# Half of two projections moved from plain tiles into a Strassen group of a decoder layer

## The chip, the cores and the metric

One core of a Trainium2 chip. The time is the device time of one execution in microseconds; before's is the median of three runs. The kernel works in fp32, and every product is made of three matmuls on operands split into a high and a low part.

## The reference

A hybrid decoder layer on 512 tokens of width 2048:

```
z = rms_norm(x) @ w_in                 # q k v g_attn c_b c_c c_h g_conv
y_attn = window_attention(q, k, v, sinks) * silu(g_attn)
y_conv = c_b * conv3(c_c * c_h) * silu(g_conv)
x = x + concat(y_attn, y_conv) @ w_out
x = x + sigmoid(rms_norm(x) @ w_ple_gate + b) * rms_norm(p @ w_ple_proj)
```

q has 16 heads and k and v have 4, of width 64; a query sees 128 keys. g_attn, c_b, c_c, c_h and g_conv are 1024 wide each. conv3 is a causal convolution over three tokens with weights of its own for each channel.

## The kernel before, in words

**Plain tiles.** k and v come first (L276). Then 8 tiles of q and 16 tiles of c_c and c_h are made by gemm_tile: one tile is 128 output columns by 512 tokens, 16 steps over the width with three matmuls each (mm3, L155 to L157), so 48 matmuls into a PSUM bank psg. Channels lie on the partitions and tokens along the free side. The weights of four steps are one split: ACT casts them to wh (L117), DVE takes the residue wl (L118); splits are prepared three ahead.

**The clock of that stage.** gemm_tile calls tick() after every second step, so a tile is 8 ticks of six matmuls. at(when, fn) hangs work on a tick; TensorE runs exactly in the order in which the program issues it, while a scheduler sets the order of the other engines here. The work hung on ticks: the turning of k and v, the sums of squares of q's heads (half_sums, L205) and the scale from them (head_scale, with a power step on POOL, L229), and attention.

**Attention** is 16 units (4 key heads by 4 blocks of 128 queries; the first block of a head has half the keys). scores (at `when`): 8 matmuls into pss, four passes on DVE that scale, mask and take the minimum (L457), four exponentials on ACT (L462), the sums, and the scaling of the rows, two on ACT (L472) and two on DVE (L474). turn (6 ticks later): transposes into pst, a cast on ACT (L487) and a residue on DVE (L488). values (9 ticks later): matmuls into pso, a copy to `up` and two stores by POOL's queue. pss and pso have one buffer, pst two. In before q ends at tick 64, and the units start 4 ticks later, 7 ticks apart, beside the c tiles.

**q tiles** cost DVE a shuffle, two rotary products, an add, a residue of the squares and two residues of q (L340 to L343, L131, L436). e_block (a small projection) sits in the middle of four of them, E_AT. h_forms prepares, for one eighth of the width, the sums of blocks of x that the next stage needs, and stores them by POOL's queue (8 sets, one behind each of eight tiles).

**c tiles.** For a pair of tiles, DVE makes zc = c_c times the squared inverse norm (L664), u = zc * c_h (L670), ACT the first tap (L672) and DVE two more (L674); the result goes to conv_dram. The last pair is finished behind the stage.

**Strassen groups.** The rest is 7 groups: three over w_mid (c_b with g_conv twice, then g_attn), two over w_out, two over w_ple_gate. A group makes 1024 columns for 512 tokens by the seven products of Strassen's scheme on 2 x 2 blocks: 28 steps (PER) of 12 matmuls (run_step, L846). Here tokens lie on the partitions. Each step needs a split of 128x1024 (L812 on ACT, L813 on DVE, two steps ahead) and some of them a sum of weight blocks (L794 to L800, or an adding DMA by POOL's queue, add_block). From here on every engine runs in the order of the program; soon(before or after, step) hangs work on a step. `quarters` joins the products into the four quarters of a group; conv_group and attn_group then turn them back to channels on partitions (turn, L912, 16 transposes in two calls).

Of the kernel before, what the change touches and what calls it, by code (L numbers as in the profile page):

```python
# [35 lines left out]
def hymba_layer(ctx: ExitStack, tc: tile.TileContext, io):  # L36
# [268 lines left out]
    with ExitStack() as att:  # L305
# [107 lines left out]
        def q_tile(t):  # L413
            ps = product()
            sq = split_tile(squares(ps))

            def sum_q():
                if t % 4 == 0:
                    tok["q"] = ps_o.tile([P, T], F32, name="pso")
                half_sums(tok["q"], sq, t % 4, t % 4 == 0, t % 4 == 3)  # L420
                if t % 4 == 3:
                    tok["q"] = take_rows(tok["q"], 8)

            def scale_q():
                sl = nscale[:, :, 2 * t - 6 : 2 * t + 2]
                head_scale(tok["q"], sl, tok["x", -1], nc.gpsimd)()

            at(clock[0] + 6, sum_q)
            if t % 4 == 3:
                at(clock[0] + (9 if t == 3 else 17), scale_q)  # L430
            qr = rotate(ps, qg)
            for hf in range(2):
                own, oth = slice(hf * HD, hf * HD + HD), slice((1 - hf) * HD, (1 - hf) * HD + HD)
                st = big.tile([P, T], F32R, tag="big", name="qst")
                nc.scalar.copy(st[own], qr[own])
                nc.vector.tensor_tensor(st[oth], qr[own], f32(st[own]), op=ALU.subtract)  # L436
                qst[2 * t + hf] = st
# [223 lines left out]
        for i in range(8):  # L661
            ps = product()
            zc = cw.tile([P, T], F32, tag="cw", name="zc", bufs=4) if i < 7 else rowp.tile([P, T], F32, tag="rows", name="zc")
            tt(zc, ps, rx2, op=ALU.mult)  # L664
            if i == 7:
                break
# [39 lines left out]

    groups = [(io["w_mid"], n) for n in range(3)] + [(io["w_out"], n) for n in range(2)] + [(io["w_ple_gate"], n) for n in range(2)]
    NG = len(groups)
    chunks = [(0, 1, 2, 3)] * 3 + [(0, 1, 3, 2), (0, 1, 2, 3), (0, 1, 3, 2), (0, 1, 3, 2)]
    LATE = (3, 5)  # L710
    T1_BY_DMA, T3_BY_DMA = range(1, NG - 1), (2, 3, 4)
    steps = []
# [13 lines left out]
    PER = len(steps) // NG  # L726
    HS, MIX, GATE = 0, 3 * PER, 5 * PER

# [90 lines left out]
    def run_step(s, forms):  # L819
# [10 lines left out]
        if start and first:  # L830
            if (g, acc) == (NG - 1, "a"):
                ps = [ps_t.tile([P, T], F32, name="pst") for _ in range(2)]
            else:
                ps = ps_abc[("abc".index(acc) + g) % 3].tile([P, 2, T], F32, name="psp")
                if g >= 5:
                    ps = [ps[:, b] for b in range(2)]
            psum[g, acc] = ps
        ps = psum[g, acc] if g >= 5 else [psum[g, acc][:, b] for b in range(2)]
        wh, wl = weights[s]
# [20 lines left out]
        else:  # L860
            for t in range(2):
                products(t)
        if g in (2, 4, 6):
            for i in range(2):
# [64 lines left out]
    def quarters(g, qs, s0):  # L929
# [12 lines left out]
        soon(after, s0 + 26, lambda: join(qs[0, 0], g, "c", ALU.add))  # L942

    def conv_group(g):
        s0, q, yc = g * PER, {}, []
# [12 lines left out]
        def load_y(i):  # L958
            yc.append(itile("yc"))
            nc.sync.dma_start(yc[i], conv_dram[4 * g + i])  # L960

        def evict(j, i, pt):
            y = yc[2 * j + i]
            tt(y, pt, y, op=ALU.mult)
            nc.gpsimd.dma_start(mix_dram[4 * g + 2 * j + i], y)

# [63 lines left out]
    def out_group(g):  # L1030
        s0, first = g * PER, 2 * (g - 3)

# [54 lines left out]

    s1, s2 = 4 * PER, 5 * PER
    for j, when, plan in (
# [27 lines left out]
    def gate_group(g):  # L1117
# [3 lines left out]
        def load_b():  # L1121
            ext["b"] = itile("gb")
            nc.sync.dma_start(ext["b"], io["b_ple_gate"][2 * (g - 5)][:, 0])

# [6 lines left out]
        def add_b(t, n):  # L1131
            nc.gpsimd.dma_start(q[t, n], io["b_ple_gate"][2 * (g - 5) + n], accum_op=ALU.add)

# [11 lines left out]
        def load_e(t, n, tile=itile):  # L1145
            ext[t, n] = [tile("e") for _ in range(2)]
            for b in range(2):
                nc.sync.dma_start(ext[t, n][b], e_dram[t][2 * (g - 5) + n][:, b])

# [7 lines left out]
        def add_x2(t, n):  # L1157
            nc.gpsimd.dma_start(q[t, n], x2_dram[t][2 * (g - 5) + n], accum_op=ALU.add)

        def store(t, n):  # L1160
            nc.gpsimd.dma_start(part(out, t, 2 * (g - 5) + n), q[t, n])

# [20 lines left out]
        soon(after, s0 + 22, load_b)  # L1183
        soon(after, s0 + 22, load_e, 0, 0, itile if g == 5 else spare)

        def new_z():
            q[1, 0] = qtile("z")

        if g == 5:
            soon(after, s0 + 26, join, 0, 0, "c", r_2)  # L1190
# [47 lines left out]
    attn_group(2)  # L1238
    out_group(3)
    out_group(4)  # L1240
    gate_group(5)
    gate_group(6)


# [6 lines left out]
    def last_conv():  # L1251
        tt(u, ps, zc, op=ALU.mult)
        nc.vector.tensor_scalar(y, u, convw[:, 2, 7:], None, op0=ALU.mult)
        for s in (1, 0):
            n = 2 - s
            stt(y[:, n:], u[:, : T - n], convw[:, s, 7:], y[:, n:], op0=ALU.mult, op1=ALU.add)
        nc.gpsimd.dma_start(conv_dram[7], y)

# [45 lines left out]
def _layout(inputs):  # L1304
# [15 lines left out]
    def cols(v):  # L1320
# [60 lines left out]
```

## Time and profile before

| | us |
|---|---|
| runs | 939.81, 940.88 (median), 943.29 |
| profiled execution, time | 940.36 |
| its span on the core | 938.6 |

The profile is of one execution. Busy time of a group is what its instructions cover together; a mean is the duration of one, and neighbours on an engine overlap a little. "Idle before" is what the engine waited in front of them, with what ended the wait. The chain that ended last is followed back from the last instruction.

### The profile page before, as it was taken

What the parts mean: (1) busy time and instruction counts of PE and PEld (TensorE: products, weight loads), DVE (VectorE), ACT (ScalarE), POOL (GpSimd) and SP (SyncE); (2) the same over time, 40 slices, a digit from 0 to 9 for tenths busy, and PEclk for the clock granted to TensorE, in tenths of its full rate; (3) what the DMA queues carried; (4) which work ended last, traced back from release to release, by engine and by line L of the source; (5) the groups of instructions that cost most, each with busy time, mean ns of one, the idle gap of its engine ahead of it and who ended that gap; (6) DMA issues with size and microseconds to landing.
All of it is one profiled execution on the core that took longest, in us unless ns stands there. A gap on an engine that the chain in (4) does not pass through costs nothing.

```text
span 938.6 us, 12350 instructions
## 1 busy us (share of the span) xinstructions
PE 929.7 (99%) x4292; PEld 773.0 (82%) x4292; DVE 714.9 (76%) x1108; ACT 525.2 (56%) x891; POOL 147.3 (16%) x196
## 2 busy tenths in 40 slices
PE   9999999999999999999999999999999999999997
PEld 7888888888888888888888888888888888888885
DVE  6778868875766676668667768989768696999777
ACT  7646555665656665245444446655556576665442
POOL 2002142051212221000100120011120112001101
PEclk9999999999999999999999999999999999999999
DMA  8434456454554667865924887785996995578757
GB/s 313 154 104 157 146 185 228 160 164 128 131 167 145 181 179 238 306 202 178 248 90 142 255 222 239 239 234 159 292 331 182 227 293 146 135 236 268 180 135 212
DMA packets 67502, 186.12 MB, mean 198 GB/s; under 512 B 8080, under 2 KB 14528, under 8 KB 67440
## 3 DMA queue, kind: packets, MB, share of 16 engines
q1 hardware_dynamic: 46192, 128.47, 40.2%
q0 software_dynamic: 21104, 56.86, 26.0%
q8 instruction: 33, 0.54, 0.2%
q14 instruction: 29, 0.24, 0.1%
q10 hardware_dynamic: 144, 0.01, 0.0%
HBM read 155.95 MB, written 29.36 MB: 197 GB/s over the span
## 4 chain that ended last, share of the span: by engine, by line
PE 96%; DVE 2%; issue 1%; DMA 0%; ACT 0%; SPq 0%; DVEq 0%; ACTq 0%
PE psp L846 51%; PE psg L155 9%; PE psg L157 9%; PE psg L156 9%; PE pst L846 3%; PE pss L276 2%; PE pst L276 2%; PE pst L912 1%; PE pst L482 1%; PE pss L556 1%; PE pst L556 1%; PE pss L450 1%; PE pss L449 1%; PE pso L497 1%; PE pso L496 1%
## 5 line engine op out<-in xcount | busy, mean ns | idle before, releaser
L846 PE MATMUL psp<-wh,form 128*128 128x512 f32 x1056 | 326.5, 390 | 0.3 <-DVE form L578 0.3
L846 PEld LDWEIGHTS psp<-wh,form 128*128 128x128 f32 x1056 | 197.4, 188 | 41.0 <-DVE form L578 0.7
L846 PE MATMUL psp<-wl,form 128*128 128x512 f32 x528 | 205.5, 389 | 0.0
L155 PE MATMUL psg<-hsh,wh 128*128 128x512 f32 x384 | 152.2, 396 | 0.0
L157 PE MATMUL psg<-hsh,wl 128*128 128x512 f32 x384 | 149.8, 390 | 0.0
L156 PE MATMUL psg<-hsl,wh 128*128 128x512 f32 x384 | 149.8, 390 | 0.0
L813 DVE TENSOR_TENSOR wl<-wy,wh 128x1024 fp32r<-128x1024 f32 x84 | 102.6, 1222 | 45.5 <-ACT wh L812 44.9
L812 ACT CAST wh<-wy 128x1024 fp32r<-128x1024 f32 x84 | 88.3, 1051 | 79.6 <-PE psp L846 61.4
L118 DVE TENSOR_TENSOR wl<-raw,wh 128x512 fp32r<-128x512 f32 x120 | 82.3, 688 | 46.3 <-ACT wh L117 28.4
L846 PEld LDWEIGHTS psp<-wl,form 128*128 128x128 f32 x528 | 99.1, 188 | 20.6
L117 ACT CAST wh<-raw 128x512 fp32r<-128x512 f32 x120 | 73.6, 616 | 65.0 <-PE psg L156 51.4
L813 DVE TENSOR_TENSOR wl<-wx,wh 128x1024 fp32r<-128x1024 f32 x56 | 68.4, 1223 | 31.9 <-ACT wh L812 31.7
L812 ACT CAST wh<-ws 128x1024 fp32r<-128x1024 f32 x56 | 59.1, 1055 | 59.1 <-PE psp L846 34.6
L812 ACT CAST wh<-wx 128x1024 fp32r<-128x1024 f32 x56 | 58.8, 1052 | 57.9 <-PE psp L846 49.4
L813 DVE TENSOR_TENSOR wl<-ws,wh 128x1024 fp32r<-128x1024 f32 x56 | 68.5, 1222 | 23.7 <-ACT wh L812 23.6
L157 PEld LDWEIGHTS psg<-hsh,wl 128*128 128x128 f32 x384 | 72.1, 188 | 15.5
L155 PEld LDWEIGHTS psg<-hsh,wh 128*128 128x128 f32 x384 | 72.2, 188 | 14.0
L156 PEld LDWEIGHTS psg<-hsl,wh 128*128 128x128 f32 x384 | 72.2, 188 | 13.8
L846 PE MATMUL psp<-wh,hsh 128*128 128x512 f32 x192 | 75.0, 391 | 0.0
L846 PE MATMUL psp<-wl,hsh 128*128 128x512 f32 x192 | 74.7, 389 | 0.0
L846 PE MATMUL psp<-wh,hsl 128*128 128x512 f32 x192 | 74.7, 389 | 0.0
L798 DVE TENSOR_TENSOR wy<-wy,ws 128x1024 f32<-128x1024 f32 x56 | 68.2, 1218 | 0.0
(223 smaller groups left out, 1351.3 us busy)
## 6 DMA issues: line engine op xcount, KB each, us to landing
raw<-in_w_in SPq DMA_DIRECT2D x48, 512.0 KB, 3.6
ws<-in_w_mid SPq DMA_DIRECT2D x24, 512.0 KB, 4.3
h<-hf POOLq DMA_DIRECT2D x32, 256.0 KB, 4.3
wx<-in_w_mid SPq DMA_DIRECT2D x16, 512.0 KB, 4.5
wx<-in_w_out SPq DMA_DIRECT2D x16, 512.0 KB, 6.4
ws<-in_w_out SPq DMA_DIRECT2D x16, 512.0 KB, 5.4
ws<-in_w_ple_gate SPq DMA_DIRECT2D x16, 512.0 KB, 5.0
wy<-in_w_mid SPq DMA_DIRECT2D x12, 512.0 KB, 6.2
```

Source lines behind the costliest of these rows:

```text
L117: nc.scalar.copy(wh, raw)
L118: nc.vector.tensor_tensor(wl, raw, f32(wh), op=ALU.subtract)
L155: nc.tensor.matmul(ps, wh, ah, start=first, stop=False)
L156: nc.tensor.matmul(ps, wh, al, start=False, stop=False)
L157: nc.tensor.matmul(ps, wl, ah, start=False, stop=last)
L276: nc.tensor.matmul(kv_ps[t], w[:, t, :], a, start=k == 0 and i == 0, stop=k == KT - 1 and i == 2)
L449: nc.tensor.matmul(sc[:, r, lo:], q, khh[j][:, ks], start=True, stop=False)
L556: nc.tensor.matmul(banks[t], a, w, start=k == 0 and i == 0, stop=k == 1 and i == 2)
L798: tt(y, y, got[g, "s1" if f == 6 else "s0", c], op=ALU.add)
L812: nc.scalar.copy(wh, src)
L813: tt(wl, src, f32(wh), op=ALU.subtract)
L846: nc.tensor.matmul(ps[t], a, w[:, i], start=start and first and i == 0 and n == 0, stop=last and i == 1 and n == 2, skip_group_check=not s ...
```

## The change

The second halves of c_c and c_h (4 tiles each) leave the plain tiles and become a Strassen group of their own, the first of now eight: its left 512 columns are c_c, its right 512 are c_h. square_group joins the quarters, multiplies c_c by c_h and the squared inverse norm token by token on DVE (L952 in the changed kernel), turns the product to channels (turn at steps 30 and 32, that is in the next group's third and fifth step), and takes the convolution straight from PSUM: ACT the last tap, DVE the two others in place (L960, L963), then a store to conv_dram by POOL's queue.

With 8 c tiles less there are 56 ticks fewer for attention. Its units now start at tick 46, inside q's tiles, 6 ticks apart up to the fourth, then from tick 67 on 42/11 ticks apart. The forms (h_forms) come behind tiles 0 to 5, 9 and 12, and e_block one tile earlier. Indices of groups move up by one.

```
-    E_AT = (2, 3, 4, 5)
+    E_AT = (1, 2, 3, 4)
...
-            at(c0 + 36 + 16 * t, finish_v)
+            at(c0 + 36 + 8 * t, finish_v)
...
-        busy[0] = [load_p]
-        for j, i in enumerate((4, 6, 7, 11, 14, 16, 18, 20)):
+        load_p()
+        for j, i in enumerate((0, 1, 2, 3, 4, 5, 9, 12)):
             busy.setdefault(i, []).append(lambda j=j: h_forms(j))
+        for u in range(NKV * NB):
+            attention(u // NB, u % NB, c0 + (46 + 6 * u if u < 4 else 67 + 42 * (u - 4) // 11))
         for t in range(8):
             q_tile(t)
-        t0 = clock[0] + 4
-        for u in range(NKV * NB):
-            attention(u // NB, u % NB, t0 + 7 * u)
-        for i in range(8):
+        for i in range(4):
             ps = product()
...
-    groups = [(io["w_mid"], n) for n in range(3)] + ...
+    groups = [(io["w_mid"], n) for n in range(4)] + ...
...
+    def square_group(g):
+        s0, q = g * PER, {}
+        quarters(g, q, s0)
+        def times(t, src):
+            for b in range(2):
+                stt(q[t, 0][:, b], src()[:, b], column(rx2_tok, t, b), q[t, 1][:, b], op0=ALU.mult, op1=ALU.mult)
+        def last():
+            q[1, 0] = qtile("z")
+            times(1, lambda: psum[g, "a"])
+        def evict(f, pt):
+            y = itile("yconv")
+            nc.scalar.activation(y, pt, AF.Copy, scale=convw[:, 2, f : f + 1])
+            for s in (1, 0):
+                n = 2 - s
+                stt(y[:, n:], pt[:, : T - n], convw[:, s, f : f + 1], y[:, n:], op0=ALU.mult, op1=ALU.add)
+            nc.gpsimd.dma_start(conv_dram[f], y)
+        soon(after, s0 + 27, times, 0, lambda: q[0, 0])
+        soon(after, s0 + 28, last)
+        for j in range(2):
+            soon(after, s0 + 30 + 2 * j, lambda j=j: turn(
+                j, (q[0, 0], q[1, 0]), lambda i, pt: evict(4 + 2 * j + i, pt)))
...
-    conv_group(0)
+    square_group(0)
     conv_group(1)
...
-        "w_mid": blocks(columns(TCB, TGC, TCB + 4, TGC + 4, TGA, TGA + 4)),
+        "w_mid": blocks(columns(TCC + 4, TCH + 4, TCB, TGC, TCB + 4, TGC + 4, TGA, TGA + 4)),
```

How the order of instructions moves is shown at three places. The first is DVE's queue ahead of the second attention unit's scores (ptl_a is the residue of unit 0's turned block, prob the scores); before:

```order
L118 TENSOR_TENSOR wl<-raw,wh 128x512
L664 TENSOR_TENSOR zc<-psg,rows_xx 128x512
L118 TENSOR_TENSOR wl<-raw,wh 128x512 x2
L488 TENSOR_TENSOR ptl_a<-pst,pth_a 128x512
L457 ISA prob,negm<-pss,mask,nsink,nscale 128x256
```

And now:

```order
L490 TENSOR_TENSOR ptl_a<-pst,pth_a 128x512
L580 TENSOR_TENSOR hf<-g,hf 128x512
L580 TENSOR_TENSOR hf<-g,hf 128x256
L340 STREAM_SHUFFLE shf<-psg 128x512
L131 TENSOR_TENSOR sl<-sqh,sh 128x512
L341 SCALAR_TENSOR_TENSOR rot<-psg,q_norm_gain,cos 128x512
L342 SCALAR_TENSOR_TENSOR shf<-shf,q_norm_gain,sin 128x512
L459 ISA prob,negm<-pss,mask,nsink,nscale 128x256
L459 ISA negm 128x1
L343 TENSOR_TENSOR rot<-rot,shf 128x512
```

Between the residue and the unit's first score pass there now stand two residues of forms and four steps of a q tile, where there was nothing. Behind the score passes follow two residues of q, the small steps with a split, and the shuffle of the next q tile ahead of the scaling.

The second is ACT's queue in the late units (pth_a is the cast of a turned block, the exponentials write sums); before:

```order
L462 ACTIVATE prob,sums<-prob,negm 128x256 x4
L467 ACTIVATE sk<-sk 128x4
L117 CAST wh<-raw 128x512
L472 ACTIVATE prob<-prob,sums 128x256 x2
L499 COPY up<-pso 128x512
L117 CAST wh<-raw 128x512 x2
L487 CAST pth_a<-pst 128x512 x2
```

And now:

```order
L464 ACTIVATE prob,sums<-prob,negm 128x256 x2
L117 CAST wh<-raw 128x512
L464 ACTIVATE prob,sums<-prob,negm 128x256 x2
L469 ACTIVATE sk<-sk 128x4
L501 COPY up<-pso 128x512
L474 ACTIVATE prob<-prob,sums 128x256 x2
L489 CAST pth_a<-pst 128x512 x2
```

Before, the casts behind a unit's scaling are those of the same unit's turned block; now its turn comes after the next unit's scores, and the casts that follow a scaling are those of the unit before it.

The third is DVE's queue where a group's product is turned and evicted, beside the next group's weights (yc and yconv are the evicted tiles); before:

```order
L813 TENSOR_TENSOR wl<-wy,wh 128x1024
L964 TENSOR_TENSOR yc<-pst,yc 128x512 x2
L813 TENSOR_TENSOR wl<-wy,wh 128x1024
L964 TENSOR_TENSOR yc<-pst,yc 128x512 x2
L798 TENSOR_TENSOR wy<-wy,ws_4515 128x1024
```

And now, behind the new group:

```order
L814 TENSOR_TENSOR wl<-wy,wh 128x1024
L963 SCALAR_TENSOR_TENSOR yconv<-pst,conv_w,yconv 128x511
L963 SCALAR_TENSOR_TENSOR yconv<-pst,conv_w,yconv 128x510
L963 SCALAR_TENSOR_TENSOR yconv<-pst,conv_w,yconv 128x511
L963 SCALAR_TENSOR_TENSOR yconv<-pst,conv_w,yconv 128x510
L814 TENSOR_TENSOR wl<-wy,wh 128x1024
L799 TENSOR_TENSOR wy<-wy,ws_3921 128x1024
L814 TENSOR_TENSOR wl<-wy,wh 128x1024
```

Four taps stand between two splits instead of two products, and two splits and a weight sum lie between the halves instead of one split.

More of the change, by code (lines that the diff above doesn't have):

```diff
@@ L429, in q_tile @@
             if t % 4 == 3:
-                at(clock[0] + (9 if t == 3 else 17), scale_q)
+                at(clock[0] + 9, scale_q)
             qr = rotate(ps, qg)
@@ L704, in qtile @@
         return quad.tile([P, 2, T], F32, tag="q", name=name)
[L707 removed]
+    groups = [(io["w_mid"], n) for n in range(4)] + [(io["w_out"], n) for n in range(2)] + [(io["w_ple_gate"], n) for n in range(2)]
     NG = len(groups)
[L709 to L711 removed]
+    chunks = [(0, 1, 2, 3)] * 4 + [(0, 1, 3, 2), (0, 1, 2, 3), (0, 1, 3, 2), (0, 1, 3, 2)]
+    LATE = (4, 6)
+    T1_BY_DMA, T3_BY_DMA = range(1, NG - 1), (3, 4, 5)
     steps = []
@@ L834, in run_step @@
                 ps = ps_abc[("abc".index(acc) + g) % 3].tile([P, 2, T], F32, name="psp")
-                if g >= 5:
+                if g >= NG - 2:
                     ps = [ps[:, b] for b in range(2)]
             psum[g, acc] = ps
-        ps = psum[g, acc] if g >= 5 else [psum[g, acc][:, b] for b in range(2)]
+        ps = psum[g, acc] if g >= NG - 2 else [psum[g, acc][:, b] for b in range(2)]
         wh, wl = weights[s]
@@ L1030, in out_group @@
     def out_group(g):
-        s0, first = g * PER, 2 * (g - 3)
+        s0, first = g * PER, 2 * (g - 4)
         def new(t, n):
@@ L1131, in add_b @@
         def add_b(t, n):
[L1132 removed]
+            nc.gpsimd.dma_start(q[t, n], io["b_ple_gate"][2 * (g - 6) + n], accum_op=ALU.add)
         def join(t, n, acc, r):
@@ L1183, in gate_group @@
         soon(after, s0 + 22, load_b)
-        soon(after, s0 + 22, load_e, 0, 0, itile if g == 5 else spare)
+        soon(after, s0 + 22, load_e, 0, 0, itile if g == 6 else spare)
         def new_z():
             q[1, 0] = qtile("z")
-        if g == 5:
+        if g == 6:
             soon(after, s0 + 26, join, 0, 0, "c", r_2)
```

41 lines of the change are left out of this document (22 added, 19 removed).

## The prediction

> **What bounds the kernel now.** I read the page's busy shares first, then TensorE's waits, then the chain of work that ended last, then the windows of the attention stage.
>
> ```profile
> span 938.6 us, 12350 instructions
> PE 929.7 (99%) x4292; PEld 773.0 (82%) x4292; DVE 714.9 (76%) x1108; ACT 525.2 (56%) x891; POOL 147.3 (16%) x196
> ```
>
> ```profile
> PE pso L190 <- DVE zeros L186: 1.1, 1, 1.1
> PE pss L276 <- ACT wh L117: 0.6, 1, 0.6
> PE psp L846 <- DVE form L578: 0.3, 1, 0.3
> ```
>
> TensorE is busy 99% of the span, and in the whole run it waits three times, for 2.0 us together. So the time is the sum of what stands in TensorE's queue, and its price is the distance between two starts, not the mean duration of a matmul. The chain of waits gives that distance:
>
> ```profile
> 303.53 0.87 PE pst L482 x8
> 315.83 0.87 PE pst L482 x8
> 371.83 0.23 PE psg L157
> 383.39 0.23 PE psg L157
> 383.61 84.32 PE psp L846 x372
> 467.94 0.87 PE pst L912 x8
> ```
>
> In the last plain tile's stretch the L157 rows at 371.83 and 383.39 are 51 matmuls apart: 0.2267 us each. In the grouped stage 372 matmuls take 84.32 us: 0.2267 again. Eight transposes take 0.87 us. Two transposes of neighbouring attention units are 12.30 us apart.
>
> ```profile
> 180.00:366.00 186.00, 186.00 (x936) 156.94 (x934) 129.72 (x348) 116.35 (x303) 47.83 (x64) 1.00 0.56 156
> ```
>
> This window holds before's attention stage (columns: length, PE, PEld, DVE, ACT, POOL, clock, DMA share). PE has no gap in 186 us, DVE is busy 70%, ACT 63%, and the granted clock is 1.00. There is idle time on the two vector engines there, and the change spends it.
>
> **TensorE's sum.** Eight plain tiles go: 8 x 48 = 384 matmuls x 0.2267 = 87.04 us. One group of 28 steps x 12 = 336 matmuls comes: 76.16 us. Its product has to be turned, 16 transposes: 1.74 us. Attention, q, k and v keep their matmuls. Net: -9.14 us. The Trainium skill prices this otherwise: TensorE: Matmul & The Clock Gate, section Back-to-back issue gap, gives about 131 ns per 512-column matmul in a sustained stream, or N/2.4 + 2.5 = 216 ns by its formula; by 131 ns the 48 matmuls less would bring 6.3 us, and the sum would be -4.6. The trace says 226.7 ns, near the formula and far from 131, and the trace's number stands.
>
> **Attention, pulled together.** A tick is six matmuls, 1.36 us. A unit came every 7 ticks: 9.52 of the 12.30 us, so its own TensorE work is 2.78. Now late units come every 42/11 = 3.82 ticks: 5.19 + 2.78 = 8.0 us. What must fit beside it, from before's groups by form:
>
> ```profile
> L118 DVE TENSOR_TENSOR wl<-raw,wh 128x512 fp32r<-128x512 f32 x120 | 82.3, 688 | 46.3 <-ACT wh L117 28.4 <-PE pst L276 8.7 <-PE pst L482 6.5
> L457 DVE CUSTOM_DVE_ANT_0 prob<-pss,mask,nsink 128x256 f32<-128x256 f32 x48 | 23.3, 541 | 4.4 <-PE pss L450 4.3
> L488 DVE TENSOR_TENSOR ptl_a<-pst,pth_a 128x512 fp32r<-128x512 f32 x28 | 18.2, 685 | 6.3 <-ACT pth_a L487 6.3
> L474 DVE TENSOR_SCALAR prob<-prob,sums 128x256 f32<-128x256 f32 x24 | 7.5, 353 | 0.4
> L469 DVE RECIPROCAL sums<-sums 128x4 f32<-128x4 f32 x16 | 2.8, 178 | 0.5
> L468 DVE TENSOR_TENSOR sums<-sums,sk 128x4 f32<-128x4 f32 x16 | 2.6, 162 | 6.3 <-ACT sk L467 6.1
> L674 DVE SCALAR_TENSOR_TENSOR yconv<-u,conv_w,yconv 128x512 f32<-128x512 f32 x14 | 10.5, 750 | 1.0 <-ACT yconv L672 0.8
> L664 DVE TENSOR_TENSOR zc<-psg,rows_xx 128x512 f32<-128x512 f32 x8 | 5.5, 687 | 2.7 <-PE psg L157 2.7
> ```
>
> Busy over count gives what one costs in a row of its kind. DVE per full unit: 4 score passes x 0.485 = 1.94; three small steps 0.5; two scalings 0.62; two residues (ptl_a) 1.30: 4.37 us. Weight splits come one per two ticks: 1.91 x 0.686 = 1.31. A pair of c tiles costs two products at 0.69 and two taps at 0.75, 2.88 per 16 ticks: 0.69. Sum 6.4 of 8.0 us, plus 0.4 of waiting for ACT's exponentials at L468. ACT's side:
>
> ```profile
> L117 ACT CAST wh<-raw 128x512 fp32r<-128x512 f32 x120 | 73.6, 616 | 65.0 <-PE psg L156 51.4 <-PE pst L276 9.5 <-issue 2.7
> L462 ACT ACTIVATE prob<-prob,negm 128x256 f32<-128x256 f32 x48 | 23.9, 499 | 18.9 <-DVE negm L457 18.9
> L472 ACT ACTIVATE prob<-prob,sums 128x256 f32<-128x256 f32 x24 | 10.9, 503 | 0.0
> L487 ACT CAST pth_a<-pst 128x512 fp32r<-128x512 f32 x28 | 15.2, 588 | 8.1 <-PE pst L482 7.8
> L499 ACT COPY up<-pso 128x512 f32<-128x512 f32 x16 | 9.2, 575 | 1.0 <-PE pso L497 1.0
> ```
>
> ACT: 4 x 0.50 + 2 x 0.45 + 2 x 0.54 + 0.58 + 1.91 x 0.61 = 5.7 of 8.0. So the eleven late units fit, and I charge them nothing; the cover is 1.2 us of DVE per unit.
>
> The tight place is q's tail, where the first units stand 6 ticks apart beside q's own work.
>
> ```profile
> L340 DVE STREAM_SHUFFLE shf<-psg 128x512 f32<-128x512 f32 x8 | 5.9, 740 | 0.0
> L341 DVE SCALAR_TENSOR_TENSOR rot<-psg,q_norm_gain,cos 128x512 f32<-128x512 f32 x8 | 5.9, 743 | 0.0
> L343 DVE TENSOR_TENSOR rot<-rot,shf 128x512 f32<-128x512 f32 x10 | 6.8, 683 | 0.0
> L131 DVE TENSOR_TENSOR sl<-sqh,sh 128x512 fp32r<-128x512 f32 x10 | 6.8, 676 | 0.1
> L436 DVE TENSOR_TENSOR qst<-rot,qst 64x512 fp32r<-64x512 f32 x16 | 11.0, 686 | 3.2 <-ACT qst L435 2.7
> L578 DVE TENSOR_TENSOR hf<-g,hf 128x256 fp32r<-128x256 f32 x16 | 6.7, 421 | 0.5 <-ACT hf L577 0.4
> L578 DVE TENSOR_TENSOR hf<-g,hf 128x512 fp32r<-128x512 f32 x8 | 5.5, 692 | 1.5 <-ACT hf L577 1.1
> ```
>
> A q tile costs DVE a shuffle and two rotary products (L342 taken like L341) at 0.74, then 0.68 + 0.68 + 2 x 0.69: 4.95 us. A set of forms (h_forms) costs two residues of 0.42, one of 0.69 and four 256-wide steps, taken like the residue at 0.42: 3.2. A slot of 6 ticks is 8.16 + 2.78 and 0.45 for q's sums (two matmuls): 11.4 us. DVE has 4.37 + 3 x 0.69 + 3/4 of 4.95 = 10.1 in it, and 13.3 in the first slot, which also holds the forms of q's sixth tile. That is 1.9 us too much once.
>
> Where it lands I read from the order of instructions. Behind unit 0's last residue DVE has two form residues (1.1) and four steps of q (2.9) ahead of unit 1's scores: with that residue 4.7 us from the scores' start. Then: four passes 1.9, rotary add and two q residues 2.1, small step 0.2, split 0.7, two small 0.3, shuffle 0.7, scaling 0.6: 11.2 us. TensorE gets to unit 1's turn after scores 0.95 + 8.16 + q's sums 0.45 + unit 0's values 0.45 = 10.0 us. It waits 1.2 us. The weights for TensorE's next steps are three to four splits ahead in DVE's queue there, 8 to 11 us, so the lateness does not show in them. For the forms in two other slots, for hops between engines and for the loads and stores that h_forms now issues in every tile of q, I add 0.8 us. **Stalls: 2.0 us**; bounds: 0 (DVE's rows overlap a little, and all of it fits) and 7 (each of the first five units pays 1.2 and a load is late).
>
> The first unit also waits for its scale from POOL:
>
> ```profile
> 195.53 5.92 POOL L229 TENSOR_TENSOR msh<-msh,half_neg 128x32 f32<-128x32 f32 x1 [1.08 <-DVE msh L224]
> 197.25 0.41 DVE L597 TENSOR_TENSOR g<-xg 128x256 f32<-128x256 f32 x1
> 197.59 0.68 DVE L118 TENSOR_TENSOR wl<-raw,wh 128x512 fp32r<-128x512 f32 x1
> ```
>
> The turn that feeds it is at tick 41, unit 0's scores at 46: five ticks and one finish_v, 7.25 us. POOL's power step takes 5.9, another small one about 1, so the scale comes about when the scores end. Queued behind DVE's wait are q's rotary rows and one split. I charge nothing.
>
> **The eighth group and the joints.** Its weights, sums and joins cost DVE what the group before it costs; the page shows no wait there. New is the eviction: per half, DVE has four taps at 0.75 = 3.0 us, after TensorE's four transposes and ACT's copy (0.59, like L487). TensorE has 0.87 + 5.46 us until the step whose split stands behind these taps; DVE needs about 0.45 + 0.7 + 3.0 + 1.2 = 5.35 (split by this row):
>
> ```profile
> L813 DVE TENSOR_TENSOR wl<-wx,wh 128x1024 fp32r<-128x1024 f32 x56 | 68.4, 1223 | 31.9 <-ACT wh L812 31.7
> ```
>
> It fits by 1 us: nothing charged, 0 to 2 as bounds. POOL's four new stores stand between weight additions of two different groups, so nothing urgent is behind them.
>
> **Sum.** -9.14 + 2.0 = -7.1 us. The profiled execution took 940.36 us (span 938.6); the median, 940.88, is 0.5 above it. From the median: **933.7 us**. A measurement of this kernel can tell about 0.5%, 4.7 us: faster ends at 936.2, slower begins at 945.6.
>
> **Rivals.**
> - *It fits entirely.* For: DVE and ACT idle 30% and more in the stage, and starts are closer than durations. Against: the first slot's 13.3 us. Then 940.88 - 9.14 = 931.7. Chance 0.25.
> - *DVE becomes the bound in q's tail.* The first five units each pay unit 1's 1.2 us, and a load of h_forms, now in six tiles in a row, costs 1 more: 7 us, 938.7, no change by the bound. For: 10.1 us plus waits in 11.4 leaves little to catch up. Against: each slot after the first has room. Chance 0.17.
> - *The exchange between ACT and DVE becomes the bound in the late units: slower.* In ACT's queue the casts of a unit's turned block now stand behind the next unit's scaling. From the next scores' start this is 0.95 + 1.94 + 0.6 + 0.34 + 0.91 + 1.09 + 0.65 = 6.5 us, and 8 to 10 with the casts and splits that stand between. TensorE wants the values 5.18 ticks, one scores, one turn and one values later: 7.05 + 0.95 + 0.87 + 0.91 = 9.8. If the chain takes 11.3, each of 12 units loses 1.5: 18 us, 949.7. It decides from 10.9 us on: 12 x 1.15 = 13.8 is what separates 931.7 from 945.6. Against: DVE is at 80%, ACT at 71%. Chance 0.09.
> - *POOL's power step holds DVE*, 5.7 us before unit 0 and again before unit 8, less some 2.6 us of slack: 2 x 3.1, 939.9. Against: the three rows above; inside POOL's 5.92 us DVE's two-input steps took 0.41 and 0.68, their usual time. Chance 0.04. By the Trainium skill, SBUF — State Buffer, section Who interferes with whom, a DVE instruction with two SBUF inputs and a GpSimd instruction that reads SBUF shut each other out for a whole instruction; the trace disagrees here.
>
> **How the numbers follow.** The forecast with stalls of 1 to 4.4 us has 0.45. It and the full fit end below 936.2: faster 0.70. DVE in q's tail and POOL's hold end within the bound: same 0.21. Slower 0.09. The range goes from 930.7 (full fit, less 1 us that single runs of before lay below its median) to 939.0 (the second rival); the slower rival and the ends of the others, under 0.2, stay outside.
>
> **What would show it.** Right: TensorE's waits list a turn of attention (prob) of about a microsecond early, in q's eighth tile, little else, and the span shrinks by 7. Wrong: waits of the values matmuls on the turned blocks in every late unit (third rival); waits of psg on weight splits in q's tail (second); DVE still for 5 us while POOL computes the power (fourth); waits of the grouped matmuls on splits right after the new group.

## The result and the profile after

The changed kernel takes 952.16 us (median of 4 runs, 950.66 to 954.01) against 940.8 before: ratio 1.0118, 95% interval 1.0089 to 1.0146. It is slower by 11.4 us; forecast were 7.1 us less. The profiled execution has a span of 951.4 us against 938.6.

First the head of the page (of the changed kernel) and TensorE's waits (us in total, times, longest):

```profile
span 951.4 us, 12285 instructions
...
PE 929.6 (98%) x4260; PEld 770.6 (81%) x4260; DVE 741.2 (78%) x1115; ACT 536.7 (56%) x890; POOL 149.3 (16%) x196
```

```profile
PE pst L558 <- DVE e L550: 6.3, 1, 6.3
PE psm L219 <- ACT rowsum L210: 3.4, 2, 2.8
PE psp L847 <- DVE wl L814: 1.9, 1, 1.9
PE pso L190 <- DVE zeros L186: 1.1, 1, 1.1
PE pst L558 <- DVE vt L395: 1.0, 1, 1.0
PE pst L484 <- ACT prob L474: 0.9, 1, 0.9
PE pss L276 <- ACT wh L117: 0.8, 1, 0.8
...
```

Three waits became nine (two under half a microsecond are left out). Only one is the one forecast (unit 1's turn on prob, 0.9 us). The large ones are in places of which the prediction says nothing: the small projection in q's tile 1 (L558), the scale of the first four q tiles (L219), the fourth step of the first group (L847). The TensorE matmuls are 32 fewer, as worked out, and where attention is now dense TensorE hardly waits. The stage after, by its window (length, PE, PEld, DVE, ACT, POOL, clock, DMA share, GB/s), which answers to before's window of 180 to 366 us:

```profile
180.00:320.00 140.00, 139.11 (x721) 117.94 (x722) 105.77 (x292) 95.51 (x256) 38.78 (x45) 1.00 0.64 174
```

The 0.9 us that are missing from 140 are unit 1's turn. DVE is busy 76% there, ACT 68%.

A part of the loss that no list of waits shows is the clock. TensorE's rows (start, duration, what; timeline) at the longest wait, and the windows (columns as above) of the stretches just behind the three longest waits:

```profile
83.27 0.80 PE L558 MATMUL pst<-wh,ptsh 128*128 128x512 f32 x1 [6.26 <-DVE e L550]
83.86 0.63 PE L558 MATMUL pst<-wh,ptsl 128*128 128x512 f32 x1
84.29 0.63 PE L558 MATMUL pst<-wl,ptsh 128*128 128x512 f32 x1
```

```profile
83.20:87.30 4.10, 4.03 (x10) 3.20 (x11) 1.55 (x4) 1.82 (x4) 0.79 (x2) 0.50 0.35 131
148.80:152.20 3.40, 3.04 (x11) 2.46 (x12) 1.11 (x6) 0.60 (x2) 3.27 (x4) 0.64 0.97 270
326.20:329.90 3.70, 3.35 (x9) 2.68 (x10) 3.70 (x5) 0.31 (x1) 0.00 (x0) 0.64 0.02 8
```

The starts are 0.43 us apart instead of 0.227, and the granted clock falls to 0.50: after each of these waits 7 to 10 matmuls pay 0.2 us extra, 5 us in all. To see where the time went I took all neighbouring starts of matmuls in the trace that lie over 0.3 us apart and added up what each is above 0.227:

| place | before | after |
|---|---|---|
| start, 0 to 10 us | 1.1 | 2.9 |
| q's tile 1, small projection, 70 to 90 us | - | 10.2 |
| row sums, q's tiles 4 and 5, 140 to 165 us | - | 5.7 |
| unit 1's turn, 180 us | - | 1.2 |
| first group's start, 320 to 335 us | - | 3.8 |
| all else | 4.5 | 4.3 |
| sum | 5.6 | 28.2 |

(The parts are rounded.) -9.1 + 28.2 - 5.6 = 13.5 us. From the first start of a matmul to the last the changed kernel takes 13.8 us longer, so 0.3 us stay unexplained; behind the last start it is 1.0 us shorter, which makes the 12.8 us between the spans. So the gain by TensorE's sum is real, and 22.6 us are lost; 1.9 of them at the start, where 7 matmuls come at half clock, as in some of the other profiles and not in the rest.

**Tile 1.** DVE's and POOL's rows:

```profile
77.52 0.17 DVE L335 TENSOR_TENSOR rk<-msh,r_x 128x16 f32<-128x16 f32 x1 [0.79 <-POOL msh L229]
80.48 0.69 DVE L550 TENSOR_TENSOR e<-pss,pg 128x512 f32<-128x512 f32 x1 [2.79 <-DMA pg<-in_ple_norm_gain]
...
82.53 0.68 DVE L550 TENSOR_TENSOR e<-pst,pg 128x512 f32<-128x512 f32 x1
...
87.67 0.68 DVE L395 TENSOR_TENSOR vt<-pst,rows_x 128x512 f32<-128x512 f32 x1
```

```profile
74.19 3.30 POOL L229 TENSOR_TENSOR msh<-msh,half_neg 128x16 f32<-128x16 f32 x1 [2.42 <-DVE msh L224]
77.45 0.61 POOL L541 DMA_DIRECT2D pg<-in_ple_norm_gain  x1
```

The projection moved one tile earlier needs two pst banks, and v still holds one: its second scaling (vt) runs at 87.67, behind the projection. So the projection's third and fourth part share a bank, and TensorE waits until DVE has emptied it. DVE itself is late, since its gain row pg is loaded by POOL's queue behind k's power step.

**Row sums.** SP's, ACT's and DVE's rows around the fourth set of forms:

```profile
117.21 12.02 SPq L106 DMA_DIRECT2D raw<-in_w_in  x3
129.71 0.82 SPq L644 DMA_DIRECT2D xg<-in_x  x2
```

```profile
134.67 1.42 ACT L645 ACTIVATE xg<-xg,norm_gain 128x512 f32<-128x512 f32 x2 [1.08 <-DMA xg<-in_x]
...
148.54 0.56 ACT L210 COPY rowsum<-pso 8x512 f32<-8x512 f32 x1
```

```profile
135.43 0.42 DVE L599 TENSOR_TENSOR g<-xg 128x256 f32<-128x256 f32 x1 [1.11 <-ACT xg L645]
...
139.59 0.74 DVE L340 STREAM_SHUFFLE shf<-psg 128x512 f32<-128x512 f32 x1
```

q's tile 3, counted from 0, is finished at 127.7, its shuffle starts at 139.6: ahead of it in DVE's queue stand the forms, which wait for x, whose load stood in SP's queue behind weight loads. Behind the shuffle come the projection's products, behind them its squares on ACT, behind those the copy of the row sums that TensorE waits for. The lag from a q tile's last matmul to its shuffle, worked out from both kinds of rows, shows how DVE falls behind:

| q tile | 0 | 1 | 2 | 3 | 4 | 5 | 6 | 7 |
|---|---|---|---|---|---|---|---|---|
| before, us | 4.9 | 1.2 | 1.3 | 1.3 | 6.7 | 3.7 | 4.0 | 4.9 |
| after, us | 5.5 | 4.8 | 7.8 | 11.9 | 13.6 | 8.3 | 2.6 | 1.1 |

Before's forms stood behind tiles 4, 6 and 7 of q. How full DVE is there, by windows of q's tiles 2 to 4 (the columns as above; after the length come PE, PEld and DVE):

```profile
92.00:110.00 18.00, 18.00 (x83) 14.89 (x82) 14.79 (x27) 11.98 (x26) 4.41 (x9) 1.00 0.57 188
110.00:127.00 17.00, 17.00 (x78) 14.05 (x78) 15.61 (x29) 11.82 (x24) 3.66 (x7) 1.00 0.66 240
127.00:144.00 17.00, 17.00 (x79) 14.00 (x78) 13.83 (x27) 11.26 (x21) 4.28 (x8) 1.00 0.71 232
```

DVE is busy 82, 92 and 81% in a queue that runs in order, with waits of 1.1 us and the like in it. While a set of forms comes with every tile, the lateness grows from tile to tile; it falls only from tile 5 on.

**First group.** The last convolution's rows, of after (with POOL's last stores of attention; L504 is the adding one) and of before:

```profile
321.03 0.49 DVE L1282 TENSOR_SCALAR yconv<-u,conv_w 128x512 f32<-128x512 f32 x1 [4.26 <-DMA a<-up]
```

```profile
306.26 1.07 POOL L504 DMA_DIRECT2D a<-up  x1 [7.77 <-DMA a<-up]
306.90 1.07 POOL L503 DMA_DIRECT2D a<-up  x1
312.73 1.03 POOL L504 DMA_DIRECT2D a<-up  x1 [4.75 <-DMA a<-up]
```

```profile
384.56 0.49 DVE L1253 TENSOR_SCALAR yconv<-u,conv_w 128x512 f32<-128x512 f32 x1 [0.22 <-DMA a<-up]
```

yconv lies in memory that attention's last `up` tiles hold until their stores have landed. DVE waits 4.26 us for them, and the weight sums and splits stand behind it in its queue. The last unit itself ends as far ahead of the group as before: its copy to `up` is done 12.8 us before the group's first matmul, 12.4 in the kernel before. But the last units come 6 to 8 us apart instead of some 12, and POOL's stores run into each other: each adding store waits until the unit's first store has landed (7.77 us at 306.26), and the next unit's first store stands behind it. So the last adding store is issued 9.7 us after the copy, where before it was 6.1.

### The profile page after: what moved, and what is told of

Read it like the earlier page. It is cut to its first block, busy times and chain, and to the rows that moved or that the text cites. A ratio compares the mean times of both kernels' runs of the same rounds, so it can differ in the third digit from the quotient of the medians.

```text
span 951.4 us, 12285 instructions
## 1 busy us (share of the span) xinstructions
PE 929.6 (98%) x4260; PEld 770.6 (81%) x4260; DVE 741.2 (78%) x1115; ACT 536.7 (56%) x890; POOL 149.3 (16%) x196
## 4 chain that ended last, share of the span: by engine, by line
PE 76%; issue 2%; DVE 2%; DMA 2%; ACT 1%; POOL 0%; SPq 0%; DVEq 0%; POOLq 0%; ACTq 0%
PE psp L847 59%; PE pst L847 3%; PE psg L155 3%; PE psg L156 3%; PE psg L157 3%; PE pst L913 2%; DMA e<-e 1%; PE pst L484 1%; DMA a<-up 1%; PE pss L452 1%; PE pss L451 1%; PE pso L498 1%; PE pso L499 1%; ACT prob L464 0%; DVE wy L795 0%
## 5 line engine op out<-in xcount | busy, mean ns | idle before, releaser
L847 PE MATMUL psp<-wh,form 128*128 128x512 f32 x1152 | 356.1, 390 | 0.0
L847 PEld LDWEIGHTS psp<-wh,form 128*128 128x128 f32 x1152 | 215.5, 188 | 44.4 <-DVE form L580 0.4
L847 PE MATMUL psp<-wl,form 128*128 128x512 f32 x576 | 224.3, 389 | 0.0
L847 PEld LDWEIGHTS psp<-wl,form 128*128 128x128 f32 x576 | 108.1, 188 | 22.7 <-DVE wl L814 0.2
L155 PE MATMUL psg<-hsh,wh 128*128 128x512 f32 x256 | 103.0, 402 | 0.0
L847 PE MATMUL psp<-wl,hsh 128*128 128x512 f32 x256 | 100.5, 392 | 1.9 <-DVE wl L814 1.9
L156 PE MATMUL psg<-hsl,wh 128*128 128x512 f32 x256 | 101.2, 395 | 0.0
L157 PE MATMUL psg<-hsh,wl 128*128 128x512 f32 x256 | 100.8, 394 | 0.0
L847 PE MATMUL psp<-wh,hsh 128*128 128x512 f32 x256 | 100.5, 393 | 0.0
L847 PE MATMUL psp<-wh,hsl 128*128 128x512 f32 x256 | 100.2, 392 | 0.0
L847 PEld LDWEIGHTS psp<-wl,hsh 128*128 128x128 f32 x256 | 48.4, 189 | 12.4 <-DVE wl L814 2.3
L157 PEld LDWEIGHTS psg<-hsh,wl 128*128 128x128 f32 x256 | 48.8, 191 | 10.7
L155 PEld LDWEIGHTS psg<-hsh,wh 128*128 128x128 f32 x256 | 48.9, 191 | 9.4
```

What stands on the lines that cost most here:

```text
L155: nc.tensor.matmul(ps, wh, ah, start=first, stop=False)
L156: nc.tensor.matmul(ps, wh, al, start=False, stop=False)
L157: nc.tensor.matmul(ps, wl, ah, start=False, stop=last)
L847: nc.tensor.matmul(ps[t], a, w[:, i], start=start and first and i == 0 and n == 0, stop=last and i == 1 and n == 2, skip_group_check=not s ...
```

## The experiments

Times are medians beside the kernel before of the same chip; the ratio is to it. All but e8 and e9 start from the changed kernel.

**Each place by itself (e1 to e3), and together (e4).**

```
e1  -    E_AT = (1, 2, 3, 4)
    +    E_AT = (2, 3, 4, 5)
e2  -        for j, i in enumerate((0, 1, 2, 3, 4, 5, 9, 12)):
    +        for j, i in enumerate((0, 1, 2, 4, 5, 7, 9, 12)):
e3  -    u, y = itile("u"), itile("yconv")
    +    u, y = (rowp.tile([P, T], F32, tag="rows", name=n) for n in ("u", "yconv"))
e4  = e1 + e2 + e3
```

> The changed kernel with one line taken back: the small projection (e_block) sits again in q's tiles 2 to 5 and not 1 to 4. Theory (the loss is local: in tile 1 the projection comes before v's second bank is free and before its gain row is loaded, TensorE stands 0.95 and 6.26 us there, and 10 matmuls behind it come 0.427 instead of 0.227 us apart, 2.0 us): 9.2 us less, about 943, and TensorE's waits no longer list the 6.3 us on e. Rival (DVE has too much to do in q's tiles with the forms and the early attention units, so the debt only shows elsewhere): under 3 us less, 949 or above, and a new wait of about the same size in q's tiles 5 to 7, where the last projection now meets the first attention unit. Rival (the dense attention or the new group makes the kernel slow): no change, 952.

Measured: 952.76 us, ratio 1.0125 (1.0098 to 1.0152), no gain. TensorE's waits of e1:

```profile
PE pso L205 <- ACT sh L130: 4.2, 1, 4.2
PE psp L847 <- DVE wl L814: 3.5, 1, 3.5
PE psm L219 <- ACT rowsum L210: 3.5, 2, 2.8
PE pss L451 <- DVE e L550: 3.3, 1, 3.3
```

The 6.3 us on e are gone and four others stand in their place; lags of q's tiles 1 to 4 are 10.4, 13.6, 17.8 and 12.2 us. The theory of three separate places falls: with the forms in every tile DVE is behind throughout q, and what TensorE waits for is whatever comes next.

> The changed kernel with the forms of x behind tiles 0, 1, 2, 4, 5, 7, 9 and 12 instead of 0 to 5, 9 and 12, so that none stand between q's tile 3 and the scale of the first four q tiles. Theory (DVE does these forms from 135.4 to 139.6 us ahead of tile 3's rotary rows, the products of the small projection in tile 4 come late, ACT's copy of the row sums stands behind their squares, and TensorE waits 3.1 and 0.7 us and then has 8 matmuls at half clock, 1.6 us): 5 us less, about 947; the 6.3-us wait on e early in q and the 1.9-us wait at the first group stay. Rival (the copy is late because of the small projection in tile 4 alone, which stands where it stood before): no change, 952. Rival (dense attention or the new group): no change, and the forms moved among the attention units cost 1 to 3 us more.

Measured: 951.21 us, ratio 1.0094 (1.0066 to 1.0121). The 2.8 us on the row sums are gone, but the wait at the first group grew from 1.9 to 4.0 us, and 0.8 of a unit's scores came anew. Undecided by itself; again a wait moves on.

> The changed kernel with the two tiles of the last convolution (u and yconv, in front of the first group) taken from rows that are long dead instead of memory that attention's last output tiles hold until POOL's adding stores have landed. Theory (DVE waits 4.26 us for such a store at 320.5 us, the weight sums and splits stand behind it in its queue, TensorE waits 2.3 us at the first group and has 8 matmuls at half clock, 1.6 us): 3.6 us less, about 948.5. Rival (the first weights of the group are late by themselves, since their loads reuse memory of the same stage): under 1 us less, and DVE's weight sum waits for a DMA in its place. Rival (dense attention or the new group): no change.

Measured: 948.14 us, ratio 1.0074 (1.0056 to 1.0092): 4 us less, as expected, and the wait on wl is no longer in the list. Mended alone, this place gives what was expected. Its size hangs on what goes before, though: where the memory is not touched, the same wait is 4.0 us in e2, 0.4 in e13 and absent in e5.

> The three edits together: the small projection in tiles 2 to 5, no forms behind tile 3, the last convolution's tiles in free memory. Theory (the arithmetic gain of 9.1 us is real, and all that took it away are the three places and the half clock behind each): 952.2 - 9.2 - 5.3 - 3.6 = 934, faster than the kernel before by 0.7%, with TensorE's waits at 3 us in sum or less. Rival (DVE's debt moves on to the next tight place): 940 or above. Rival (the dense attention or the new group costs the time): 945 or above with no single wait above 2 us.

Measured: 942.37 us, ratio 1.0013 (1.0004 to 1.0022), 8 us above the theory's number. One long wait is left, of unit 0's scores on the bank of the last projection, which now meets them in tile 5:

```profile
PE pss L451 <- DVE e L550: 5.8, 1, 5.8
```

**Forms out of q's tiles (e5), bank and gain row (e6), both with the free memory (e7).**

```
e5  -        for j, i in enumerate((0, 1, 2, 3, 4, 5, 9, 12)):
    +        for j, i in enumerate((5, 7, 8, 9, 10, 11, 12, 13)):
e6  -            at(clock[0] + 12 + t, scale_v)
    +            at(clock[0] + 11 + t, scale_v)
    -            nc.gpsimd.dma_start(pg, io["ple_norm_gain"][:, n * T : (n + 1) * T])
    +            nc.sync.dma_start(pg, io["ple_norm_gain"][:, n * T : (n + 1) * T])
e7  = e5 + e6 + e3
```

> The changed kernel with all forms of x moved behind tiles 5 and 7 to 13: none in q's tiles 0 to 4. The first theory (three separate places) has lost e1. Theory now (DVE's arrears: the forms stand in DVE's queue between a finished q tile and its rotary rows, with waits for the loaded x in between, and the small projection's products behind them come late, wherever it sits): no wait on the row sums at the scale of the first four q tiles (5.2 us with its half clock gone), the wait on e in tile 1 about halved (some 4 us gone); the first group's wait stays or grows: about 943. Rival (attention and forms do not fit together in the late units: DVE has 1.2 us free per unit and a set of forms takes 3.2): the waits in q go, but waits of scores or turns of 1 us and more come in most units with forms, 948 or above. Rival (the small projection in tile 1 is late through its bank and gain row alone): the 6.3-us wait stays whole, 947.

Measured: 936.4 us, ratio 0.9943 (0.9927 to 0.9960): 16 us less than the changed kernel by one line, nearly twice what was expected, and faster than before. Its waits (parts), and the stage of attention, up to the first group, with seven of the eight sets of forms now in it:

```profile
PE pst L558 <- DVE e L550: 3.2, 1, 3.2
...
PE pst L558 <- DVE vt L395: 0.4, 1, 0.4
```

```profile
163.00:303.00 140.00, 140.00 (x727) 118.74 (x727) 117.78 (x333) 109.26 (x290) 50.94 (x66) 1.00 0.69 197
```

All lags in q are 1.1 to 1.7 us. TensorE has no gap in these 140 us, with DVE busy 84% and ACT 78%: the rival of the crowded late units falls. The wait at the first group went too, though its memory was not touched: the last adding store is issued 5.2 us after the copy here (9.7 in the changed kernel). Why the stores landed sooner is open.

> The changed kernel with the scaling of v one tick earlier (both of v's banks are given free ahead of the small projection in tile 1) and the projection's gain row loaded through SP's queue instead of POOL's, where it stands behind k's power step; the forms stay. If the 6.3-us wait in tile 1 is a matter of bank and gain row alone: it goes, and with the later waits as they were the time is about 943. If DVE's arrears from the forms are what counts: the wait in tile 1 goes, but the time saved is lost again at the next places in q (tile 2 to 5, row sums, first scores), as when the projection was moved: 948 or above.

Measured: 943.68 us, ratio 1.0028 (1.0018 to 1.0037). 8.5 us less, so this wait, unlike in e1, does not come back in full: the row sums went from 2.8 to 3.6 us.

> Together: no forms in q's tiles 0 to 4 (behind 5 and 7 to 13), v's banks one tick earlier, the gain row through SP, the last convolution's tiles in free memory. Theory (the arithmetic gain of 9.1 us is real; forms in q's tiles, the bank, and the memory of the last convolution took it away): 952.2 - 9.2 - 5.2 - 4.0 = 934, no wait of TensorE above 2 us behind the start, no matmuls at half clock. Rival (eight sets of forms beside the close attention units are too much for DVE): 940 or above, with waits of scores and turns in the late units.

Measured: 935.09 us, ratio 0.9933 (0.9918 to 0.9948), as the theory has it; no half clock behind the start.

**Parts of the change put alone into the kernel before.** e8: E_AT = (1, 2, 3, 4). e9: forms behind (0, 1, 2, 3, 4, 5, 9, 12).

> The kernel before with one line of the change alone: the small projection in q's tiles 1 to 4 instead of 2 to 5 (its forms stay where they were, the first behind tile 4). If bank and gain row alone make the wait in tile 1: some 6 to 9 us slower than before, 947 to 950. If it takes the forms behind tile 0 as well: under 3 us slower, 944 or less.

Measured: 949.83 us, ratio 1.0092 (1.0072 to 1.0112), 8.1 us slower, without a set of forms anywhere near:

```profile
PE pst L556 <- DVE e L548: 6.2, 1, 6.2
```

> The kernel before with one line of the change alone: the forms of x behind tiles 0 to 5, 9 and 12, as the change has them; no new group, attention where it was, the small projection in tiles 2 to 5. Theory (the forms in q's tiles cost by themselves, since they stand in DVE's queue ahead of a finished tile's rotary rows): TensorE waits for row sums and squares in q's tiles 3 to 5 as in the run with the projection moved later (4.4, 0.6 and 3.0 us, and 15 matmuls at half clock, 3.0 us): 8 to 11 us slower than before, 949 to 953. Rival (the forms hurt only because the attention units come close behind): under 3 us slower, 944 or less.

Measured: 956.03 us, ratio 1.0155 (1.0137 to 1.0174), 15.6 us slower. More than expected, since the squares of tile 0 are late as well (4.2 us at 75 us):

```profile
PE pso L205 <- ACT sh L130: 5.4, 3, 4.2
PE psm L219 <- ACT rowsum L210: 3.8, 1, 3.8
PE pso L206 <- DVE sl L131: 1.1, 2, 0.7
```

The lags are 12.9, 8.6, 12.0, 14.3 and 13.2 us. Attention is far away in this kernel, so its closeness is not what makes the forms dear.

**Which of the two in tile 1 (e10: the scaling of v alone; e11: the gain row alone).**

> The changed kernel with v's scaling one tick earlier alone; the gain row stays on POOL's queue behind k's power step. If the bank makes the wait (the projection's third and fourth parts share one bank while v holds the other): the 6.3 us go although DVE's products are still late, 944. If the late gain row makes it: DVE frees the pss bank late and TensorE waits for that instead, 948 or above.

Measured: 945.29 us, ratio 1.0048 (1.0030 to 1.0065). The 6.3 us on e go though pg is as late as ever; the row sums' wait rises to 4.2, the first group's to 2.8.

> The changed kernel with the gain row through SP's queue alone; v's scaling stays behind the projection. If the bank makes the wait: the wait shrinks by the 2.8 us that DVE waited for the row, 3.5 us stay, with or without half clock: 947.5 to 949.5. If the late gain row makes it: the wait goes, 944.

Measured: 946.98 us, ratio 1.0060 (1.0042 to 1.0078), just below the range expected by the bank. Of its waits:

```profile
PE psm L205 <- ACT sh L130: 3.5, 1, 3.5
PE pst L558 <- DVE e L550: 3.4, 1, 3.4
```

3.4 us of the 6.3 stay. The bank makes the wait, the gain row makes it longer by 2.9. The wait on squares (L205) is new; the loss moves on here too.

**The best version.** e12 is e7 and one step more:

```
-            second = head_scale(tok["k"], rk, tok["x"], nc.vector)
+            second = head_scale(tok["k"], rk, tok["x"], nc.gpsimd)
```

> The fastest so far (forms late, bank, gain row, last convolution) and one step more: the product behind k's power step is done by POOL and not by DVE, which waits 3.0 us for POOL there with v's scaling behind it. Theory: TensorE's two waits on vt in tile 1 (gaps of 0.84 and 0.86 us, 1.2 us over a usual distance) go: 1.2 us less than that kernel, about 934 beside a kernel before at 941. Rival (DVE is late there through its own work): no difference.

Measured: 932.76 us, ratio 0.9905 (0.9887 to 0.9923), the fastest of all. The head of its page and all of TensorE's waits:

```profile
span 931.5 us, 12277 instructions
...
PE 922.4 (99%) x4260; PEld 767.0 (82%) x4260; DVE 737.2 (79%) x1114; ACT 535.1 (57%) x890; POOL 148.2 (16%) x193
```

```profile
PE pso L190 <- DVE zeros L186: 1.1, 1, 1.1
PE psm L219 <- ACT rowsum L210: 0.6, 1, 0.6
PE pss L276 <- ACT wh L117: 0.6, 1, 0.6
```

Dense attention, the eighth group and its eviction are all in it, and TensorE waits 2.3 us in the whole run.

**Why early forms are dear (e13 to e15).** h_forms was cut in two: its loads of x are issued one tile ahead of its work (e13, from the changed kernel). e14 is e12 with the forms as the change has them; e15 is e14 with the loads ahead.

```
+            if i:
+                busy.setdefault(i - 1, []).append(lambda j=j: h_load(j))
+            else:
+                h_load(j)
             busy.setdefault(i, []).append(lambda j=j: h_forms(j))
```

> The changed kernel with the forms where they are, but each set's two loads of x issued one tile earlier. Lag is the time from the last matmul of a q tile to DVE's shuffle of it. If the forms hurt because their loads stand late in SP's queue, behind weight loads that wait for a buffer (the load of the second set is issued at 87.6, 4.9 us before its tile ends, that of the fourth at 129.7, 2.7 us after): lags in q's tiles 1 to 5 of 6 us or less instead of 4.8 to 13.6, the 5 us at the row sums go, and the wait in tile 1 stays: 945 to 948. If it is DVE's work and its hand-offs with ACT that stand ahead of the rotary rows: lags stay, 950 or above.

Measured: 945.8 us, ratio 1.0047 (1.0032 to 1.0062). Lags of tiles 1 to 5 are 1.6, 5.0, 7.3, 5.5 and 5.9 instead of 4.8 to 13.6 (tile 3 stays above the 6 expected), and of the 2.8 us on the row sums 0.6 are left. In tile 1 the wait stays, now mostly on v (e15, below, has the same and shows where it comes from):

```profile
PE pst L558 <- DVE vt L395: 6.2, 1, 6.2
PE pst L558 <- DVE e L550: 1.5, 1, 1.5
```

> The fastest so far (932.8) with its forms back behind tiles 0 to 5, 9 and 12: bank, gain row, last convolution and k's scale mended, the forms alone as the change has them. From the runs with one mend each: 952.2 - 8.5 - 4.1 - 1.2 = 938.4, with the wait at the row sums of about 5 us with its half clock, 5.6 us more than with the forms late. If forms in q's tiles cost only together with the late bank and gain row: 934 or less.

Measured: 942.75 us, ratio 1.0011 (0.9998 to 1.0025). Against e12 (0.9905) the early forms cost 1.06%, 10 us, with everything else mended; expected were 5.6.

> As the run before, with each set's loads of x issued one tile earlier. If late loads are what makes the early forms dear: as fast as with the forms late, 932 to 934, lags of 6 us or less. If DVE's work and hand-offs are: no faster than the run before, 938.

Measured: 940.43 us, ratio 0.9984 (0.9969 to 1.0000): by the ratios 2.5 us better than e14 (the intervals just touch), 7.4 worse than e12. Neither number expected came. The wait on q's row sums is down from 4.0 us to at most 0.6, but two around v and k have come (3.0 on vt, 1.5 on rows_x). They are this experiment's own: ACT runs in order, and the first set's scaling now waits for x ahead of the copy of rows_x, without which v can't be scaled (the copy starts at 64.35 in e14). The two rows:

```profile
62.81 0.72 ACT L651 ACTIVATE xg<-xg,norm_gain 128x512 f32<-128x512 f32 x1 [5.01 <-DMA xg<-in_x]
...
68.93 0.57 ACT L255 COPY rows_x<-psm 128x512 f32<-128x512 f32 x1
```

No set waits for x on DVE any more, and the lags of tiles 1 to 4 are 3.8, 5.5, 8.5 and 5.9 us where e14 has 7.3, 8.6, 11.7 and 13.2. By the ledger (distances of starts, as in the table above), e14 loses 6.1 us between 90 and 160 us (q's tiles 2 to 5) and e15 0.7; between 66 and 90 (tile 1) it is 2.2 and 7.9. One could think that DVE caught up while TensorE stood longer in tile 1. The changed kernel and e6 speak against it: they lose 10.3 and 2.2 us there, and their lags in tiles 3 and 4 are 11.9 and 13.6 against 11.3 and 12.7. So the late loads make the loss in tiles 2 to 5 (the changed kernel and e13 show the same, 5.9 against 0.6 us): the lag that is left, DVE's own steps, costs TensorE nothing there. The price that e15 pays in tile 1 for ACT's wait is new, so a version with early forms and nothing lost was not found.

## Why the prediction was wrong, step by step

- **TensorE's sum, -9.14 us: right.** The count fell by 32, the ledger closes with it to 0.3 us, and e12, in which TensorE waits 2.3 us in all, is 7.7 us below before (940.44 of the same chip); the ledger gives it 7.8 us of excess against before's 5.6, 1.9 of the difference at the start. The forecast 933.7 is met within 1.4 us by e12 and e7, with other tiles for the forms and the joints mended. That the 2.0 us of stalls agree with e12's 2.2 is luck: 1.9 of these are the half clock at the start.
- **"The eleven late units fit, and I charge them nothing": right.** TensorE has 139.11 of 140 us in after's stage and 140.00 of 140 in e5's, with more forms in it. The slower rival (ACT and DVE in the late units) did not happen.
- **Unit 1's turn, 1.2 us: right** (0.9 by the list of waits). POOL's power step for unit 0 cost nothing, as charged; the rival in which it holds DVE did not happen (the step takes 5.46 us at 150.27, and DVE's two-input steps inside it 0.42 to 0.69).
- **The new group and its eviction, nothing: right.** No wait stands behind 335 us.
- **"for the loads and stores that h_forms now issues in every tile of q, I add 0.8 us. Stalls: 2.0 us": wrong, and the main failure.** The working began at the first attention unit, at tick 46. Five of the eight sets of forms moved into the ticks ahead of it, and no sum was made there; that attention is far away was taken for room. The prices were at hand: a q tile with a projection is 72 matmuls, 16.3 us (17.3 in the trace, with sums of squares and the turning of k); DVE has the tile's 4.95, six splits at 0.69 and four products at 0.69 (another 6.9) in it, and 3.2 for forms: 15.0 us, and in tiles 2 and 3 the five steps of k's finish as well (3.4). Without forms it is 11.8 to 15.2. (By durations; neighbours overlap, so the windows of tiles 2 and 3 show 14.8 of 18 and 15.6 of 17 us busy.) In so full a queue a set whose x came late was not made good before the next: the term for loads was named, but sized without following SP's queue, where they stand behind weight loads (e15 has the loss of tiles 2 to 5 down from 6.1 to 0.7 us by the loads alone). Measured for the forms as a whole: 16 us by taking the forms out (e5), 15.6 by putting them alone into the kernel before (e9), 10 with all else mended (e14 against e12). The rival that was nearest had "DVE becomes the bound in q's tail"; it was in q's head.
- **e_block one tile earlier was not costed at all.** The change was told, its bank, its gain row on POOL's queue and v's scaling were not followed. It costs 8 to 9 us, in the changed kernel (e6) and in the one before (e8).
- **"The eighth group and the joints ... 0 to 2 as bounds": the joint failed.** The last units of attention come closer together, their stores pile up in POOL's queue, and the memory that is handed over at the first group was not looked at: 4 us (e3).
- **The price of a wait was taken as its length.** Behind each of the three longest came matmuls at half clock, 5 of the 22.6 us lost.
- The range ended at 939.0 since its worst case was a sum of waits in q's tail; none of the rivals held a wait ahead of attention.

The costs of the parts don't add up (16 + 8.5 + 4 is more than 22.6): the places share one lateness. Taking the forms out (e5) also halved the wait in tile 1 and ended the one at the first group; and mending one place alone can let another show, as in e1.

## What to carry to other kernels

When a change thins out one stage and moves its small jobs elsewhere, sum up the stage that receives them, tile by tile, and follow each moved job's loads through the queue that issues them: DVE, which runs in order and was 81 to 92% full here, made no lateness good while more came. For a step that comes earlier, ask who still holds its banks and its memory at the new time. And put each part of the change alone into the old kernel: two of them, one line each, showed here at once what the sum had left out.

## What the runs showed of the hardware

- **Short waits halve the clock.** In the profiled executions of all runs, distances of 3.64 us and more between two matmuls (17 of them, up to 6.69) were each followed by 4 to 14 matmuls 0.427 us apart; of seven from 2.28 to 3.61 us five were (2.28 and 3.15 in the changed kernel among them), and two were not (3.14 in e10, 3.61 in e5). One of 2.13 in e13 stands too close behind a longer one to be told apart. Below that none was, away from the start. The Trainium skill, TensorE: Matmul & The Clock Gate, section HAM oscillation, gives the rule that there be no idle time of TensorE above some 3.4 us. The trace agrees that long waits cost twice; it differs in the bound, since a distance of 2.28 us was enough at 326.5 us, where the clock in the window behind it is 0.64.
- **The start differs between profiles.** Some have 7 to 9 matmuls at half clock in the first 10 us (after, e5, e12), some have none (before, e3, e9, e14): 1.9 us between the profiled executions of before and after. All these kernels issue the same instructions in that time, so the difference does not come from what the programs issue there; each was profiled once, so how it varies in one kernel is not shown.
